# A decoder layer on one core: squares of x from a second copy, the last weights' second token half held back, and sums of activations two tiles at once

## The chip, the cores and the metric

The kernel runs on one core of one Trainium2 chip. The metric is the device time in microseconds of one execution of the program. The core's engines are PE (TensorE, matmuls), DVE (VectorE), ACT (ScalarE), POOL (GpSimd) and SP (SyncE, which here only issues DMAs). Every engine works through its own list of instructions in order and waits on semaphores.

## What is computed

One layer of a hybrid decoder for a sequence of 256 tokens with 2048 channels, all in float32, and a final norm:

```python
h = rms_norm(x, norm_mix_g)
q, k, v, xr, gr, sc_b, sc_c, sc_x, g_pre = split(h @ w_in)
y_a = moba_attention(q, k, v, rel_table) @ w_attn_o
y_b = rg_lru_branch(xr, gr, ...) @ w_lru_o
y_c = (sc_b * causal_conv3(sc_c * sc_x)) @ w_sc_o
g_a, g_b, g_c = split(sigmoid(g_pre + gate_b))
x = x + (g_a * y_a + g_b * y_b + g_c * y_c) @ w_out
h = rms_norm(x, norm_mlp_g)
x = x + square(relu(h @ w_mlp_up)) @ w_mlp_down
return rms_norm(x, final_g)
```

where `rms_norm(x, g) = x * rsqrt(mean(x*x, -1) + 1e-6) * g`. All weights together are about 300 MB.

## The kernel before

**Weights in two parts.** The weights are read once, as 512 KB blocks: 128 partitions x 2 x 512 numbers, which is 256 rows of a matrix by 512 columns. SP loads each into one of nine buffers `raw` (RAW = 9). ACT copies it into `hi` in the type fp32r (line 158), DVE takes the rest `lo` = `raw` - `hi` (line 159); there are five buffers of each (WB = 5). Activations are split in the same way. A product is then three matmuls: hi x hi, hi x lo and lo x hi. For blocks 0 to 7 `first` does the same (lines 206 and 207) and also makes the activations `h`: ACT scales a tile of x by its gains (line 363), DVE forms the rest (line 364). The order of the blocks is a list that is worked out ahead (`jobs`); `ahead` prepares blocks up to LOOK = 3 ahead of the one that is multiplied.

**Two ways to multiply.** `group` ("ws") holds the weights still and streams the activations: four PSUM banks, for every 128 x 128 piece one matmul with 512 columns (line 245) and one with 256 (line 246). The first two groups are `xr0` and `xr1`, over blocks 0 to 7 and 8 to 15; then `qk`. `pair` ("as") holds the activations still and streams 512 columns of weights (line 291), for both halves of the tokens (t = 0 and 1) and two stretches of 512 output channels (gi = 0 and 1). The pairs of the gates (`gt00` to `gt21`, one for each branch and half of the channels), of `w_out` (`wo0`, `wo1`) and of `w_down` (`dn00` to `dn31`) do half of their weights with a scheme of seven products in place of eight. Its steps ("s", numbered 1 to 7) take sums of blocks of weights, which DVE adds (line 186), and sums of activations, which `sums` makes: four steps on DVE (lines 97 to 100), a copy on ACT (`...ch`, line 102) and the rest on DVE (`...cl`, line 103). The plain weights are steps "n". `as_sequence` gives the order of the steps; after step 1 of a pair ACT copies the bank of (0, 0) into `...r1` (line 299, `gt21r` in the rows). `total` (lines 338 and 340, `xr0a` and `xr0b`) adds the two halves of a bank.

**Work beside.** Code that may run later is put into the lists `after` and `side`, from which `a_bit` takes a piece between blocks. Tile, the framework, fixes from the program the order of the instructions on each engine except SP, and adds the waits. Buffers of one tag are a pool: a new tile waits for the last use of the tile whose place it takes. `block` is a pool of 55 tiles of 128 x 512.

**The first norm.** POOL squares the tiles of x and adds them into `sqa`, eight multiplications and seven additions; six matmuls on PE (`pss`, lines 396 and 399) add over the partitions; `rsqrt` works on a tile of 128 x 258. The factor is needed from the evacuation of `xr` on.

**The end.** The final norm of x needs the sum of squares of each token over all channels, so it follows the last pair, `dn31`: ACT squares (line 842), DVE multiplies with the gains (line 843), seven small steps give the factor `r`, and eight scalings (lines 861 and 863) and eight DMAs of 256 KB follow.

Of the kernel before, what the change touches and what calls it, by code (L numbers as in the profile page):

```python
# [47 lines left out]
def as_sequence(nu, nb):  # L48
# [12 lines left out]
    return mixed((1, 2, 3, 4), n2) + mixed((5, 6, 7), n1)  # L61
# [3 lines left out]
def trunk_kernel(ctx, tc, x8, xn, pv, rows, w_in, rel, onehot, w_a, lru_w, w_l, w_s, w_out, w_up, w_down, out2):  # L65
# [70 lines left out]
    for kind, w, g, u0, nu, nb in order:  # L136
# [3 lines left out]
        else:  # L140
            seq = as_sequence(nu, nb)
# [123 lines left out]
    def pair(name, w, g, plain, mix, evac):  # L265
# [9 lines left out]
        def mixed(b, kk, m):  # L275
# [3 lines left out]
            return [x[:, at:at + P] for x in mix[b, kk]]  # L279
# [65 lines left out]
    xb, hl = [], []  # L345
# [576 lines left out]
```

## Time and profile before

| | |
|---|---|
| median of 3 runs (lowest, highest) | 1595.6 us (1593.0, 1595.79) |
| the profiled execution | 1596.78 us |
| its span on the core | 1594.7 us |
| PE busy | 1553.9 us (97%) |
| DVE, ACT, POOL busy | 82%, 55%, 5% |
| mean granted clock of PE | 0.993 of full speed |

The profile is of one execution. Its span is the time from the core's first to its last recorded event; 2.1 us of the execution's time lie around it. Busy shares are means over the whole span; the waits of an engine, and what released it, say where it stood still.

### The profile page before, as it was taken

To read this page: it belongs to the slowest core of one execution; us is meant where nothing else is said; L and a number is where in the kernel's file an instruction comes from. 1 tells how busy PE (TensorE), PEld (TensorE's weight loads), DVE (VectorE), ACT (ScalarE), POOL (GpSimd) and SP (SyncE) were. 2 spreads that over 40 slices of the span, in tenths; PEclk is the share of its full clock that TensorE was granted. 3 is DMA by queue.
4 is the path that set the end of the run, shared out by engine and by line. 5 is a ranking of instruction groups with operands and counts; after the bars stand their busy time and mean duration, and the time that the engine had idled before them with its cause. 6 is when DMAs were issued, how large, how long until landed. Compare 5 with 4: busy or idle time off the path is not lost.

```text
span 1594.7 us, 20814 instructions
## 1 busy us (share of the span) xinstructions
PE 1553.9 (97%) x7694; PEld 1302.7 (82%) x7694; DVE 1300.3 (82%) x1701; ACT 873.8 (55%) x1166; POOL 77.0 (5%) x85
## 2 busy tenths in 40 slices
PE   6999999999999999998999999999999999999996
PEld 5888888878888888786888888888888888888875
DVE  8964576998759886989799778987799679977897
ACT  4544856565545464655456655545555455545554
POOL 6021200000000000200100000000000000000000
PEclk9999999999999999999999999999999999999998
DMA  8665455465754575383754653575466654576353
GB/s 306 199 210 163 155 189 168 146 212 174 259 187 158 205 258 184 119 277 132 251 177 166 239 187 124 198 272 186 155 211 222 201 185 155 197 250 215 127 179 118
DMA packets 86421, 307.67 MB, mean 193 GB/s; under 512 B 10141, under 2 KB 10405, under 8 KB 86320
## 3 DMA queue, kind: packets, MB, share of 16 engines
q1 hardware_dynamic: 82656, 296.57, 55.7%
q0 software_dynamic: 2656, 8.45, 1.8%
q10 hardware_dynamic: 1008, 1.32, 0.3%
q8 instruction: 60, 0.98, 0.3%
q14 instruction: 41, 0.34, 0.1%
HBM read 304.20 MB, written 2.11 MB: 192 GB/s over the span
## 4 chain that ended last, share of the span: by engine, by line
PE 88%; DVE 7%; issue 2%; ACT 1%; DMA 1%; POOL 1%; SPq 0%; ACTq 0%; DVEq 0%; POOLq 0%
PE dn L291 20%; PE up L245 15%; PE gt L291 12%; PE up L246 8%; PE y L291 7%; PE wo L291 5%; PE qk L245 4%; PE v L291 3%; DVE lo L159 2%; PE qk L246 2%; PE sc L245 2%; PE sx L245 2%; DVE raw L186 1%; PE sb L245 1%; PE xr L245 1%
## 5 line engine op out<-in xcount | busy, mean ns | idle before, releaser
L159 DVE TENSOR_TENSOR lo<-raw,hi 128x1024 fp32r<-128x1024 f32 x648 | 775.2, 1223 | 229.6 <-ACT hi L158 221.6
L158 ACT ACTIVATE hi<-raw 128x1024 fp32r<-128x1024 f32 x648 | 664.8, 1055 | 533.2 <-DVE raw L186 105.5
L245 PE MATMUL up<-h,hi 128*128 128x512 f32 x1024 | 362.1, 399 | 0.0
L246 PE MATMUL up<-h,lo 128*128 128x256 f32 x1024 | 287.7, 281 | 0.0
L245 PEld LDWEIGHTS up<-h,hi 128*128 128x128 f32 x1024 | 192.4, 188 | 47.8
L291 PE MATMUL dn<-hi,U 128*128 128x512 f32 x704 | 223.6, 389 | 0.9 <-ACT hi L158 0.9
L246 PEld LDWEIGHTS up<-h,lo 128*128 128x128 f32 x1024 | 193.4, 189 | 0.1
L291 PE MATMUL gt<-hi,h 128*128 128x512 f32 x528 | 170.4, 394 | 7.1 <-ACT gt21r L299 4.0
L291 PEld LDWEIGHTS dn<-hi,U 128*128 128x128 f32 x704 | 132.0, 188 | 29.0 <-ACT hi L158 1.5
L186 DVE TENSOR_TENSOR raw<-raw,raw 128x1024 f32<-128x1024 f32 x128 | 153.7, 1218 | 0.8
L291 PE MATMUL dn<-lo,U 128*128 128x512 f32 x352 | 137.1, 390 | 0.0
L291 PEld LDWEIGHTS gt<-hi,h 128*128 128x128 f32 x528 | 99.5, 189 | 29.9 <-ACT hi L158 5.0
L291 PE MATMUL gt<-lo,h 128*128 128x512 f32 x264 | 103.8, 393 | 0.4 <-DVE lo L159 0.3
L245 PE MATMUL qk<-h,hi 128*128 128x512 f32 x256 | 91.4, 401 | 0.0
L291 PEld LDWEIGHTS dn<-lo,U 128*128 128x128 f32 x352 | 66.1, 188 | 13.9 <-DVE lo L159 0.3
L246 PE MATMUL qk<-h,lo 128*128 128x256 f32 x256 | 71.7, 280 | 0.0
L291 PEld LDWEIGHTS gt<-lo,h 128*128 128x128 f32 x264 | 50.1, 190 | 11.8 <-DVE lo L159 1.6
L245 PEld LDWEIGHTS qk<-h,hi 128*128 128x128 f32 x256 | 48.1, 188 | 12.1 <-ACT hi L158 0.6
L245 PE MATMUL xr<-h,hi 128*128 128x512 f32 x128 | 47.3, 419 | 8.3 <-DVE h L364 8.2
L246 PEld LDWEIGHTS qk<-h,lo 128*128 128x128 f32 x256 | 48.3, 189 | 0.3
L245 PE MATMUL sc<-h,hi 128*128 128x512 f32 x128 | 46.5, 402 | 0.0
L245 PE MATMUL sx<-h,hi 128*128 128x512 f32 x128 | 46.0, 402 | 0.0
(1044 smaller groups left out, 2369.3 us busy)
## 6 DMA issues: line engine op xcount, KB each, us to landing
raw<-in_w_in SPq DMA_DIRECT2D x222, 512.0 KB, 4.4
raw<-in_w_up SPq DMA_DIRECT2D x128, 512.0 KB, 4.4
raw<-in_w_down SPq DMA_DIRECT2D x128, 512.0 KB, 4.4
raw<-in_w_out SPq DMA_DIRECT2D x32, 512.0 KB, 4.7
raw<-in_w_a SPq DMA_DIRECT2D x16, 512.0 KB, 4.6
raw<-in_w_s SPq DMA_DIRECT2D x16, 512.0 KB, 4.9
raw<-in_w_l SPq DMA_DIRECT2D x16, 512.0 KB, 5.0
gb<-in_rows POOLq DMA_DIRECT2D x12, 256.0 KB, 4.8
```

Source lines behind the costliest of these rows:

```text
L158: act.activation(hi, raw, AF.Copy)
L159: dve.tensor_sub(lo, raw, hi.bitcast(F32))
L186: dve.tensor_add(t, t, add)
L245: pe.matmul(ps[j], hi[:, kk, cs], acts[k], start=(k == 0), stop=False)
L246: pe.matmul(ps[j][:, :S], lo[:, kk, cs], acts[k][:, :S], start=False, stop=(k == nk - 1))
L291: pe.matmul(ps[key], hl_[x], w2[y][:, kk], start=key not in begun, stop=end and i == 2, skip_group_check=True)
```

## The change

**Squares of x.** `first` and `start` no longer issue POOL's squares. Ahead of each of the blocks 8 to 15 SP loads a quarter of one half of the tokens of x a second time, tokens along the partitions (`xq`, 128 x 512, 256 KB), and ACT squares it with a running sum along the row (`ss1`). `first_norm` makes the factor on 128 x 2 numbers, and gets it along the other axis by two transposes on PE (`rt`, `pb`). Three empty entries are put into `after`, so that it comes three pieces later.

**Sums.** `sums` takes two tiles of 128 x 512 at once and works on 128 x 2 x 128 in its four steps and on 128 x 1024 after that; `h_sums`, the gated merge and the `up` part call it half as often. Its tiles come from a pool of their own, `six`, with six buffers of 128 x 1024, and `block` has 43 in place of 55.

**Last pair.** In `dn31` the second half of the sequence is sorted: all steps "s", then the plain weights. For the last four weights (LATE = 4) only t = 0 is multiplied at first; t = 1 follows with all four after that. The final norm is done for each t as soon as its four stretches are there, with its own four scalings and output DMAs.

```diff
-NBLK = 55
+NBLK = 43
+SIX = 6
+LATE = 4
...
-    return mixed((1, 2, 3, 4), n2) + mixed((5, 6, 7), n1)
+    end = mixed((5, 6, 7), n1)
+    return mixed((1, 2, 3, 4), n2) + (sorted(end, key=lambda s: s[0] == "n") if late else end)
...
     def sums(name, a1, a2):
 
-        c = block(f"{name}c")
-        c4 = [c[:, i * P:(i + 1) * P] for i in range(4)]
-        dve.tensor_sub(c4[0], a1[:, P:], a2[:, P:])
-        dve.tensor_sub(c4[1], c4[0], a1[:, :P])
-        dve.tensor_sub(c4[2], a1[:, :P], a1[:, P:])
-        dve.tensor_add(c4[3], a2[:, :P], c4[1])
-        hi, lo = block(f"{name}ch", F32R), block(f"{name}cl", F32R)
+        a1, a2 = (a.rearrange("p (k s) -> p k s", k=2) for a in (a1, a2))
+        c, hi, lo = (six.tile([P, 2, 512], dt, tag="six", bufs=SIX, name=f"{name}{n}")
+                     for n, dt in (("c", F32), ("ch", F32R), ("cl", F32R)))
+        c4 = [c[:, :, i * P:(i + 1) * P] for i in range(4)]
+        dve.tensor_sub(c4[0], a1[:, :, P:], a2[:, :, P:])
+        dve.tensor_sub(c4[1], c4[0], a1[:, :, :P])
+        dve.tensor_sub(c4[2], a1[:, :, :P], a1[:, :, P:])
+        dve.tensor_add(c4[3], a2[:, :, :P], c4[1])
         act.activation(hi, c, AF.Copy)
         dve.tensor_sub(lo, c, hi.bitcast(F32))
...
             job = jobs[c]
+            if KT // 2 <= c < KT:
+                t, i = divmod(c - KT // 2, 4)
+                xq.append(block(f"xq{t}{i}"))
+                sp.dma_start(xq[-1], xn[t, :, 512 * i:512 * (i + 1)])
+                act.activation(xq[-1], xq[-1], AF.Square, accum_out=ss1[:, t, i:i + 1])
...
             if what == "n":
-                for t in range(2):
+                held = n >= len(seq) - late
+                for t in range(1 if held else 2):
                     for kk in range(2):
                         product((t, gi), n, plain(2 * unit + kk, t), w2, kk, last[t, gi] == n and kk == 1)
-                keys = [(0, gi), (1, gi)]
+                keys = [(0, gi)] if held else [(0, gi), (1, gi)]
...
+        if late:
+            for n in range(len(seq) - late, len(seq)):
+                for kk in range(2):
+                    product((1, gi), n, plain(2 * seq[n][4] + kk, 1), parts[used[0] - len(seq) + n], kk,
+                            n == len(seq) - 1 and kk == 1)
+            o, op = others[1, gi] if nb else (None, None)
+            rest.append(evac(1, gi, ps[1, gi], got.get(o), op))
...
-            if i % 2:
-                q = sqa if i == 1 else block(f"sq{i}")
-                pool.tensor_mul(q, xb[i // 2], xb[i // 2])
-                if i > 1:
-                    pool.tensor_add(sqa, sqa, q)
...
     def first_norm():
-        pss = small("pss")
-        for m in range(2):
-            pe.matmul(pss[:, :S], ones, sqa[:, m * S:(m + 1) * S], start=(m == 0), stop=(m == 1))
+        v, q, w = (sc8[:, i, :2] for i in range(3))
+        r = rs1[:, S:]
+        dve.tensor_reduce(v, ss1, axis=mybir.AxisListType.X, op=OP.add)
...
+        pb = small("pb")
         for t in range(2):
-            for m in range(2):
-                pe.matmul(pss[:, S + t:S + t + 1], sqa[:, m * S + t * P:m * S + (t + 1) * P], ones[:, :1],
-                          start=(m == 0), stop=(m == 1))
-        rsqrt(rs1, pss[:, :S + 2], S + 2, "n1")
+            rt = block(f"rt{t}")[:, :P]
+            act.activation(rt, ones, AF.Copy, scale=r[:, t:t + 1])
+            pe.transpose(pb[:, t * P:(t + 1) * P], rt, ident)
+        act.activation(rsb, pb[:, :S], AF.Copy)
...
+    def final_norm(t):
+        v, q, n = (nrm[:, t, i:i + 1] for i in range(3))
+        dve.tensor_reduce(v, ss3[:, t], axis=mybir.AxisListType.X, op=OP.add)
+        act.activation(q, v, AF.Sqrt, scale=1.0 / D, bias=warm)
...
+        for i in range(4):
+            o = x2[t, i]
+            if i == 1:
+                act.activation(o, o, AF.Copy, scale=n)
+            else:
+                dve.tensor_scalar(o, o, n, None, op0=OP.mult)
+            (act if i % 2 else sp).dma_start(out2[t, :, 512 * i:512 * (i + 1)], o)
```

How the lists of the engines change at three places. First ACT at the turn from the first eight blocks to the later ones. `raw_...` and `hi_...` are the parts of one block of weights (the number is the tile's), `sc` small constants, `xr0a` the copy in the evacuation of the bank `xr_0`. Before:

```order
L206 ACTIVATE hi_296<-raw_295 128x1024
L426 ACTIVATE sc_177<-sc_177 128x8
L158 ACTIVATE hi_314<-raw_312 128x1024
L338 ACTIVATE xr0a<-xr_0_178 128x256
L158 ACTIVATE hi_352<-raw_350 128x1024
```

In the changed kernel:

```order
L217 ACTIVATE hi_280<-raw_279 128x1024
L439 ACTIVATE sc_167<-sc_167 128x8
L176 ACTIVATE xq_293,ss_78<-xq_293 128x512
L358 ACTIVATE xr0a<-xr_0_168 128x256
L164 ACTIVATE hi_298<-raw_296 128x1024
L176 ACTIVATE xq_334,ss_78<-xq_334 128x512
L358 ACTIVATE xr1a<-xr_1_169 128x256
L164 ACTIVATE hi_339<-raw_337 128x1024
L176 ACTIVATE xq_343,ss_78<-xq_343 128x512
L358 ACTIVATE xr2a<-xr_2_170 128x256
L358 ACTIVATE xr3a<-xr_3_171 128x256
```

The squares of `xq` are new, and `xr0a` to `xr3a`, which wait for PE's matmuls on the first eight blocks, now stand ahead of the `hi` of the next block instead of behind it.

Second, DVE in the pair `gt21`, where the sums of the merged activations for the first half (m0, before: m00 and m01) and the second (m1, before: m10 and m11) are made between the weights. The `raw` rows add two blocks of weights for a later step. Before:

```order
L103 TENSOR_TENSOR m10cl<-m10c,m10ch 128x512
L97 TENSOR_TENSOR m11c<-mf_6547,mf_6558 128x128
L99 TENSOR_TENSOR m11c<-mf_6547 128x128
L98 TENSOR_TENSOR m11c<-m11c,mf_6547 128x128
L186 TENSOR_TENSOR raw_00_6436<-raw_00_6436,raw_10_6761 128x1024
L100 TENSOR_TENSOR m11c<-mf_6558,m11c 128x128
L186 TENSOR_TENSOR raw_00_6454<-raw_00_6454,raw_10_6792 128x1024
L159 TENSOR_TENSOR lo_6765<-raw_00_6436,hi_6764 128x1024
L103 TENSOR_TENSOR m11cl<-m11c,m11ch 128x512
L159 TENSOR_TENSOR lo_6777<-raw_6774,hi_6776 128x1024
L302 TENSOR_TENSOR gt_6695<-gt_10_6677,gt21r_6605 128x512
```

In the changed kernel:

```order
L165 TENSOR_TENSOR lo_6709<-raw_11_6608,hi_6708 128x1024
L315 TENSOR_TENSOR gt_6705<-gt_20_6601,gt_6705 128x512
L108 TENSOR_TENSOR m0cl<-m0c,m0ch 128x1024
L103 TENSOR_TENSOR m1c<-mf_6523,mf_6534 128x2x128
L105 TENSOR_TENSOR m1c<-mf_6523 128x2x128
L104 TENSOR_TENSOR m1c<-m1c,mf_6523 128x2x128
L706 TENSOR_TENSOR gt_6724<-gt_11_6587,gt_6705 128x512
L106 TENSOR_TENSOR m1c<-mf_6534,m1c 128x2x128
L708 SCALAR_TENSOR_TENSOR gt_6724<-gt_6724,rs_166,gb_6481 128x512
L197 TENSOR_TENSOR raw_00_6421<-raw_00_6421,raw_10_6728 128x1024
L108 TENSOR_TENSOR m1cl<-m1c,m1ch 128x1024
L197 TENSOR_TENSOR raw_00_6439<-raw_00_6439,raw_10_6759 128x1024
```

`m0cl`, which before stood far ahead as `m00cl` and `m01cl`, has moved behind the two steps on `gt`, and it, the sums of m1 and `m1cl` lie ahead of the second addition of `raw`. On ACT the copy `gt21r` now stands ahead of `m1ch` (it stood behind `m11ch`). The place that `m0cl` takes in the six buffers is that of `h0ch`.

Third, the end of PE's list. `dn_00` is the bank of t = 0, `dn_10` that of t = 1, `U` the activations that are held still; `hi` and `lo` with one number belong to one block. Before, the last block is:

```order
L291 MATMUL dn_00_13765<-hi_14031,U_13391 128x512
L291 MATMUL dn_00_13765<-lo_14032,U_13391 128x512
L291 MATMUL dn_00_13765<-hi_14031,U_13391 128x512
L291 MATMUL dn_00_13765<-hi_14031,U_13407 128x512
L291 MATMUL dn_00_13765<-lo_14032,U_13407 128x512
L291 MATMUL dn_00_13765<-hi_14031,U_13407 128x512
L291 MATMUL dn_10_13857<-hi_14031,U_13391 128x512
L291 MATMUL dn_10_13857<-lo_14032,U_13391 128x512
L291 MATMUL dn_10_13857<-hi_14031,U_13391 128x512
L291 MATMUL dn_10_13857<-hi_14031,U_13407 128x512
L291 MATMUL dn_10_13857<-lo_14032,U_13407 128x512
L291 MATMUL dn_10_13857<-hi_14031,U_13407 128x512
```

In the changed kernel, from the last block's first matmul:

```order
L303 MATMUL dn_00_13661<-hi_13915,U_13287 128x512
L303 MATMUL dn_00_13661<-lo_13916,U_13287 128x512
L303 MATMUL dn_00_13661<-hi_13915,U_13287 128x512
L303 MATMUL dn_00_13661<-hi_13915,U_13303 128x512
L303 MATMUL dn_00_13661<-lo_13916,U_13303 128x512
L303 MATMUL dn_00_13661<-hi_13915,U_13303 128x512
L303 MATMUL dn_10_13753<-hi_13879,U_13043 128x512
L303 MATMUL dn_10_13753<-hi_13879,U_13059 128x512
L303 MATMUL dn_10_13753<-lo_13880,U_13059 128x512
L303 MATMUL dn_10_13753<-hi_13879,U_13059 128x512
L303 MATMUL dn_10_13753<-hi_13891,U_13075 128x512
L303 MATMUL dn_10_13753<-lo_13892,U_13075 128x512
```

Of the last block only t = 0 stands in its old place; 22 matmuls on `dn_10`, of which six are shown, follow it to the end of the list.

## Rows read from the trace of the kernel before

**Rows 1.** The head of the page: the span, and busy time, share of the span and instructions of each engine.

```profile
span 1594.7 us, 20814 instructions
PE 1553.9 (97%) x7694; PEld 1302.7 (82%) x7694; DVE 1300.3 (82%) x1701; ACT 873.8 (55%) x1166; POOL 77.0 (5%) x85
```

**Rows 2.** PE's waits: the matmuls that waited, what for, us in total, how often, and the longest.

```profile
PE xr L245 <- DVE h L364: 8.2, 1, 8.2
PE xr L246 <- DVE lo L207: 5.5, 4, 2.0
PE gt L291 <- ACT hi L158: 4.5, 7, 1.2
PE gt L291 <- ACT gt21r L299: 4.0, 1, 4.0
PE gt L291 <- DVE lo L159: 2.5, 4, 0.9
```

**Rows 3.** Stretches of the start: us from the span's start, length, busy time of each engine (x instructions), granted clock of PE, share of the DMA engines, GB/s.

```profile
20.00:25.00 5.00, 5.00 (x30) 4.19 (x29) 5.00 (x7) 2.11 (x4) 4.99 (x8) 1.00 1.03 405
25.00:30.00 5.00, 3.13 (x20) 2.47 (x19) 5.00 (x4) 0.00 (x0) 4.84 (x4) 1.00 1.03 338
30.00:35.00 5.00, 3.03 (x17) 2.39 (x17) 4.96 (x7) 0.00 (x0) 2.87 (x3) 1.00 0.60 206
35.00:40.00 5.00, 5.00 (x22) 4.24 (x21) 4.06 (x12) 2.20 (x4) 0.00 (x0) 0.66 0.69 220
```

**Rows 4.** The start by lines: duration in ns (minimum, median, maximum) with the times of the first and the last start, and from the lists of DVE and ACT in time order: start, us, instruction, and in brackets the idle time before it and what ended it.

```profile
L364 DVE SCALAR_TENSOR_TENSOR h<-x,pvt,h x16: 472/1258/1508, 6.8 to 34.3; 128x256 fp32r<-128x256 f32 x16
L207 DVE TENSOR_TENSOR lo<-raw,hi x10: 691/1266/2289, 5.4 to 35.2; 128x1024 fp32r<-128x1024 f32 x6, 128x512 fp32r<-128x512 f32 x4
L371 POOL TENSOR_TENSOR sqa<-sqa,sq x7: 1332/1355/2254, 9.1 to 31.6; 128x512 f32<-128x512 f32 x7
...
6.82 5.10 DVE L364 SCALAR_TENSOR_TENSOR h<-x,pvt,h 128x256 fp32r<-128x256 f32 x4
...
11.33 1.06 ACT L206 ACTIVATE hi<-raw 128x1024 fp32r<-128x1024 f32 x1 [1.35 <-DMA raw<-in_w_in]
35.13 0.21 ACT L426 ACTIVATE sc<-sc 128x8 f32<-128x8 f32 x1 [12.86 <-DVE sc L425]
```

**Rows 5.** PE's list in order of time, its first matmul and the ninth, the first one behind the matmuls of the first norm, and the first of `qk`. A matmul of line 246 (256 columns) follows each of line 245 (512 columns).

```profile
8.19 0.79 PE L245 MATMUL xr<-h,hi 128*128 128x512 f32 x1 [8.19 <-DVE h L364]
10.92 0.54 PE L245 MATMUL xr<-h,hi 128*128 128x512 f32 x1
...
48.43 0.48 PE L245 MATMUL xr<-h,hi 128*128 128x512 f32 x1
...
65.47 0.40 PE L245 MATMUL qk<-h,hi 128*128 128x512 f32 x1
```

**Rows 6.** By line, duration in ns: ACT's square and its read of the running sum, and PE's transposes.

```profile
L842 ACT ACTIVATE sq<-xr x8: 612/630/634, 1522.9 to 1582.0; 128x512 f32<-128x512 f32 x8
L842 ACT ACTIVATION_READ_ACCUMULATOR sq<-xr x8: 183/186/187, 1523.4 to 1582.5; 128x1 f32 x8
L726 PE MATMUL pm<-ident,gt x32: 270/272/328, 727.7 to 809.6; 128*128 128x128 f32 x32
```

**Rows 7.** A stretch of gt00 (columns as in rows 3), and two kinds of steps of `sums` on DVE.

```profile
320.00:330.00 10.00, 7.92 (x30) 4.92 (x29) 10.00 (x11) 5.70 (x7) 0.00 (x0) 1.00 0.15 52
...
734.22 0.28 DVE L97 TENSOR_TENSOR m00c<-mf,mf 128x128 f32<-128x128 f32 x1
738.43 0.68 DVE L103 TENSOR_TENSOR m00cl<-m00c,m00ch 128x512 fp32r<-128x512 f32 x1
```

**Rows 8.** A stretch of gt21, the matmuls on PE that waited there and the one with which they get short again, and ACT's copy of the bank.

```profile
745.00:755.00 10.00, 7.30 (x29) 4.94 (x28) 9.84 (x17) 4.67 (x7) 0.00 (x0) 1.00 0.88 304
...
746.85 0.50 PE L291 MATMUL gt<-lo,h 128*128 128x512 f32 x1 [0.27 <-DVE lo L159]
751.91 0.50 PE L291 MATMUL gt<-lo,h10ch 128*128 128x512 f32 x1 [0.76 <-DVE lo L159]
757.37 0.80 PE L291 MATMUL gt<-hi,h 128*128 128x512 f32 x1 [4.05 <-ACT gt21r L299]
761.81 0.56 PE L291 MATMUL gt<-hi,h10ch 128*128 128x512 f32 x1
...
756.74 0.58 ACT L299 ACTIVATE gt21r<-gt 128x512 f32<-128x512 f32 x1
```

**Rows 9.** The tail in order of time: PE's last matmul, the last small step, and the share of the DMA engines in 40 slices of 1584 to 1595 us.

```profile
1580.75 0.39 PE L291 MATMUL dn<-hi,U 128*128 128x512 f32 x1
...
1584.50 0.16 DVE L856 SCALAR_TENSOR_TENSOR r<-q,r 128x2 f32<-128x2 f32 x1
...
DMA  0000000499999999999999999999997420000000
```

**Rows 10.** Stretches of the last pair, DVE's last two `lo`, and a long run of matmuls in a pair with their count (from the chain that ended last).

```profile
1540.00:1550.00 10.00, 9.33 (x39) 6.83 (x39) 10.00 (x10) 4.50 (x7) 0.00 (x0) 1.00 0.11 29
1560.00:1570.00 10.00, 10.00 (x45) 8.09 (x44) 10.00 (x12) 5.83 (x8) 0.00 (x0) 1.00 0.28 107
...
1574.63 2.35 DVE L159 TENSOR_TENSOR lo<-raw,hi 128x1024 fp32r<-128x1024 f32 x2
...
1324.84 81.83 PE dn L291 x360
```

More of the change, by code (lines that the diff above doesn't have):

```diff
@@ L45, with as_sequence @@
 NB_GATE, NB_OUT, NB_DOWN = 2, 2, 2
-def as_sequence(nu, nb):
+def as_sequence(nu, nb, late):
     n1, n2 = ([("n", 0, 0, i, u) for u in range(2 * nb, nu)] for i in range(2))
@@ L72, in trunk_kernel @@
     blk = ctx.enter_context(tc.tile_pool(name="blk", bufs=1))
+    six = ctx.enter_context(tc.tile_pool(name="six", bufs=1))
     wts = ctx.enter_context(tc.tile_pool(name="wts", bufs=1))
@@ L135, in trunk_kernel @@
     uses = []
-    for kind, w, g, u0, nu, nb in order:
+    last_pair = len(order) - 1
+    for n, (kind, w, g, u0, nu, nb) in enumerate(order):
         if kind == "ws":
@@ L140, in trunk_kernel @@
         else:
-            seq = as_sequence(nu, nb)
+            seq = as_sequence(nu, nb, n == last_pair)
             uses.append(seq)
@@ L263, in group, with pair @@
         after.extend(r for r in rest if r)
-    def pair(name, w, g, plain, mix, evac):
+    def pair(name, w, g, plain, mix, evac, late=0):
         follow("as", w, g)
@@ L278, in mixed @@
             at = (m - 2) * P
-            return [x[:, at:at + P] for x in mix[b, kk]]
+            return [x[:, kk, at:at + P] for x in mix[b]]
         for n, s in enumerate(seq):
@@ L344, in trunk_kernel @@
     pvt = const.tile([P, NPV], F32, name="pvt")
-    xb, hl = [], []
+    xb, hl, xq = [], [], []
+    ss1 = const.tile([P, 2, 4], F32, name="ss1")
     ones = const.tile([P, P], F32, name="ones")
@@ L351, in trunk_kernel @@
     act.activation(warm, ones[:, :1], AF.Exp)
-    sqa = block("sqa")
     def load(eng, i, n):
@@ L475, in evac @@
             b = total(ps, f"xr{g}")
+            if g == 0:
+                after.extend([lambda: None] * 3)
             def rest():
@@ L603, in h_sums @@
         for b in range(NB_GATE):
-            for kk in range(2):
-                a = block(f"ha{b}{kk}")
-                for i in range(2):
-                    h = hl[4 * b + 2 * i + kk].bitcast(F32)
-                    dve.tensor_add(a[:, i * S:(i + 1) * S], h[:, :S], h[:, S:])
-                hm[b, kk] = sums(f"h{b}{kk}", a[:, :S], a[:, S:])
-                yield
+            a = [block(f"ha{b}{i}") for i in range(2)]
+            for i in range(4):
+                h = hl[4 * b + i].bitcast(F32)
+                dve.tensor_add(half(a, i), h[:, :S], h[:, S:])
+            hm[b] = sums(f"h{b}", *a)
+            yield
     beside(h_sums())
@@ L734, in rest @@
                     if gi < NB_OUT:
-                        for kk in range(2):
-                            mm[gi, kk] = sums(f"m{gi}{kk}", *(f[:, kk * S:(kk + 1) * S] for f in mf))
+                        mm[gi] = sums(f"m{gi}", *mf)
                 return rest
@@ L818, in evac @@
                 U.append(o)
-                if gidx >= NB_DOWN or j < 2:
+                if gidx >= NB_DOWN or j < 3:
                     return
                 def rest(gidx=gidx, uf=uf):
-                    um[gidx, j - 2] = sums(f"u{part}{gidx}{j}", half(uf, j - 2), half(uf, j))
+                    um[gidx] = sums(f"u{part}{gidx}", *uf)
                 return rest
@@ L843, in evac @@
                     dve.tensor_mul(o, o, gf[i])
[L844 to L864 removed]
+                    done.append(t)
+                    if done.count(t) == 4:
+                        final_norm(t)
+            pair(f"dn{part}{p2}", w_down, 2 * p2, lambda k, t: in_two(U[k], t), um, evac,
+                 late=LATE if part == PARTS - 1 and p2 else 0)
 def _onehot():
```

45 lines of the change are left out of this document (15 added, 30 removed).

## The prediction

> **What bounds the kernel now.** The header of the page first: TensorE (PE) is busy for 97% of the span, the vector engine (DVE) 82%, the scalar engine (ACT) 55% [rows 1]. So nothing is gained by taking work off DVE or ACT in general; a gain has to be PE waiting less, PE doing less, or the parts before PE's first and after its last matmul becoming shorter. The list of PE's waits says where it waits: 8.2 us before its first matmul, 5.5 us for second parts (`lo`) at the start, 4.5, 4.0 and 2.5 us inside the gate pairs `gt` [rows 2]. The stretches of the start show why PE waits there: from 20 to 35 us DVE is busy all the time, PE is busy 3.13 and 3.03 of 5 us, and right after that the granted clock of a 5 us stretch is 0.66 [rows 3]. Last, the end: PE's last matmul ends at 1581.14, the span at 1594.7; a chain of small steps, eight scalings and eight output DMAs lie between [rows 9].
>
> The profiled execution took 1596.78 us: span 1594.7 plus 2.1 around it. The runs shown have their median at 1595.6, 1.2 below it. I make the sum against 1596.78 and carry the difference over to the median. About 0.2% (3.2 us) is what a measurement of this kernel can tell from no change.
>
> **First norm.** The change removes fifteen GpSimd instructions (seven additions with a median of 1.355 us, eight squares). While they run, DVE's `h` step takes 1258 ns in the median; its shortest, once the last of them has ended, takes 472 ns [rows 4]. So I cost DVE's start anew with 0.45 us per `h` and 1.2 us per `lo`, 2.1 us for one block of weights, against about 3.9 now (two `h` at 1.26 and a `lo` of 1.2 to 2.3). PE needs 5.68 us for two blocks: 48 pairs of matmuls took from 48.43 to 65.47, which is 0.355 us each [rows 5], and two blocks are 16 pairs. 4.2 us of DVE for 5.68 us of PE: PE is then the slower one and stops waiting after its first blocks. Walking through it: the first `h` step starts at 6.82 [rows 4] and ends at about 7.4 with the semaphore, so PE begins 0.8 us earlier than at 8.19; its first 16 pairs take 16 x 0.355 and 1.3 more for the low clock (four pairs from 8.19 to 10.92 [rows 5]) and end at 14.5; three more groups of 16 end at 31.6; two waits of 0.25 and 0.8 us follow, because ACT now has the evacuation `xr0a` ahead of `hi` of block 8 (order shown above) and `xr0a` waits for PE; four groups more and two transposes (0.27 us each at most [rows 6]) end at 55.7. Now the same point, the first `qk` matmul, is at 65.47 [rows 5]. In these 9.8 us are also the six matmuls of `pss`, which go, and the low clock at 35 to 40.
>
> What the new work costs: eight squares on ACT, 0.63 + 0.19 us each by the same operation at the end of the kernel [rows 6]. ACT has nothing to do from 22.3 to 35.1 (its idle time of 12.86 us [rows 4]), so these 6.6 us are covered; were they not, each would push its block by 0.8 us. The copies `xq` are 2.1 MB on SP's queue, each ahead of the block with the same number, behind raw 7. The DMA engines are full up to 25 us (share 1.03, 405 GB/s), and then fall to 0.60 to 0.69 [rows 3]: the copies go into that gap. The small vectors of the norm are ready at about 47.4 by this walk and PE wants them at 51.85, so they are covered by 4.4 us. Not covered is this: GpSimd, without its squares, issues the four `lw` loads (1.1 MB) at about 3 to 7 us instead of 20.4, when the engines are full. Bounds: nothing, if they go in turn behind blocks that PE doesn't wait for; 1.1 MB at 405 GB/s, 2.6 us, if every byte delays a block that PE waits for. I take 1.0, nearer to nothing, since of the blocks that these loads meet only 2 and 3 are wanted at once. The Trainium skill (DMA: Bandwidth & Descriptors, "Issuing engines are not separate DMA queues") says that all queues interleave on the same sixteen engines; by that alone it would be the 2.6. First norm: -9.8 + 1.0 = **-8.8** (bounds -9.8 and -7.2).
>
> **Sums of two tiles at once.** Twelve calls instead of 24. Two old calls cost DVE eight steps and two `lo`: 0.28 and 0.68 by the rows [rows 7], 0.2 and 0.6 from start to start, since each begins a little before the last has ended: 2.8 us. A `lo` of twice the size takes 1.14 from start to start (two together 2.35 [rows 10], one by itself 1.21), so 512 elements more are 0.54 and 128 more 0.135: one new call costs four steps of 0.335 and a `lo` of 1.14, 2.5 us. DVE saves 0.3 per call, or nothing if the three-dimensional form runs slower. Eight of the calls (`up`) lie where PE never waits, so they are worth nothing. Two lie ahead of gt00: there DVE is busy 10.00 of 10 us and PE only 7.92, so PE is bound by it and gets what DVE saves in two calls [rows 7]: **-0.6**; bounds 0, and -2.1 (all that PE loses there). Two lie in gt21. There PE now waits 0.27 + 0.76 + 4.05 us and then works at the low clock until 761.81, ten matmuls in 4.44 us instead of 2.3 (0.227 each, by 81.83 us for 360 [rows 10]): 7.2 us in all [rows 8]. The 4.05 is a wait for ACT's copy `gt21r`, ready at 756.74 + 0.58, which stands on ACT behind the last of the sums. In the new order `gt21r` is ahead, so this wait goes. What is late next: the sums have six buffers of their own, so `m0cl` has to wait on DVE until PE has used `h0ch` for the last time (752.75 by my walk), and behind it on DVE stand the four steps of m1, two steps on `gt` and the addition that makes the next weights. From 752.75: 1.2 + 1.5 + 1.3 + 1.1 gives 757.7 for the addition, 758.7 for its `hi`, 761.1 for its `lo`. PE, by the same walk, wants them from 756.85 on: waits of 1.85, 0.8 and 1.1, 3.8 in all. That leaves 7.2 - 3.8 = 3.4, or 1.3 if the clock falls as it does now. I take **-2.5**; bounds 0 (the new buffers take it all) and -4.5 (no wait at all before the next weights but the second).
>
> **Last pair and tail.** After PE's end T the chain to `r` takes 3.5 us, then eight scalings and 2.1 MB of output, which the DMA engines carry for some 6 us [rows 9]. With the first token half already out, 1.05 MB are left: half the transfer, -3.0. But the pair is a stretch in which DVE has 10.00 of 10 us [rows 10]: the last `lo` ends at 1576.98. Now PE needs it 11 matmuls before T, 2.5 us, at 1578.65, so it is 1.7 us early. In the new order 27 matmuls follow its first use (27 x 0.227 = 6.1 us), and DVE's list before it is as long as it was: T can't be before 1576.98 + 6.1 + 0.1 = 1583.2, 2.1 us later than now; 1.8 to 2.8 with the earlier `raw` additions. So -3.0 + 2.4 = **-0.6** (bounds -1.2 and -0.2). PE would wait in three pieces for `lo`. In 1540 to 1550 PE lost 0.67 us and kept its clock at 1.00; at 25 to 35 it lost 3.8 us and at 35 to 40 the clock was 0.66 [rows 3, 10]. The expected 2 to 3 us lie between the two. The Trainium skill (TensorE: Matmul & The Clock Gate, "A second HAM failure mode: psum-queue depth-cycling") says that frequent short idling makes the clock swing to the half and back without any one long gap; by that rule the low clock comes here. It is a rival below.
>
> **Sum.** -8.8 - 0.6 - 2.5 - 0.6 = -12.5: 1584.3 against the profiled execution, **1583.1** against the median.
>
> **Rivals.**
> *The start is bound by transfers.* Copies and `lw` together are 3.2 MB more in a stretch that is full up to 25 us. For it: `hi` of block 2 already waits 1.35 us for its transfer [rows 4]. Against: 40% of the engines are free after 30 us. Were half of the start's gain lost (4.4 us), the time is 1587.5. Chance 0.15.
> *Six buffers are too few.* If `m0cl` waits for PE and PE for what stands behind it, all of gt21's gain goes and the second pass of it (m1) costs another 1 to 2 us: -12.5 + 2.5 + 1.5, 1587.1. For it: DVE has next to no idle time from 745 to 755 (9.84 of 10 us busy [rows 8]) to make it up. Against: that order takes the 4.05 us wait out for certain. Chance 0.13.
> *The last pair falls to the low clock.* The low stretch of 4.44 us at gt21 cost 2.1 us [rows 8]; the same here: 1585.2. Chance 0.14.
> *Slower: the squares hold ACT.* `hi` of blocks 8 to 15 stands on ACT behind the square of its copy. Copies and blocks are 6.3 MB, queued from about 21 us. PE wants the last at 50; the kernel is slower than now by 0.2% only if it comes 12.5 + 3.2 = 15.7 us late, at 66: a rate under 6.3 MB / 45 us = 140 GB/s. The rows show 206 to 220 where the queue was half empty and 405 where it was full [rows 3], so this is unlikely: 1600 at 135 GB/s. Chance 0.04. At 206 GB/s the last block comes at 52, near the forecast.
> *It hardly does anything*, since PE's start was set by transfers all along (`h` gets faster, PE doesn't): -12.5 + 8.8 + 1, 1592.9. Chance 0.06.
>
> **Numbers.** The forecast has 0.48. All cases except the last two are faster by more than 3.2 us: faster 0.90, the same 0.06, slower 0.04. Range: all gains at their better bound (-9.8, -2.1, -4.5, -1.2) give 1578.0; PE's waits in the gate pairs are 11.0 us [rows 2], 5.1 in gt21 and 2.1 in gt00, and of the 3.8 in the other four one may go with DVE's work: 1577. The rivals reach 1587.5, two of them together 1590. So 1577 to 1590.
>
> **What would show it.** In the new trace: GpSimd nearly idle in the first 40 us, `h` at 0.45 to 0.5 us, PE's waits for `lo` in `xr` under 1.5 us in all, the first `qk` matmul at 56 to 58, no low clock at 35 to 40. No wait of PE for `gt21r`, but one for `hi` or `lo` of about 2 us behind it. PE's last matmul at about 1571.5, the end 10.5 us after it instead of 13.6. It is wrong if `qk` starts after 60 (DMA rows then show `raw` or `xq` landing late), or if PE loses over 5 us in the last pair.

## The result and the profile after

The changed kernel takes 1580.5 us in the median (1579.2 to 1580.7), the kernel before, on the same chip, 1594.3; the ratio is 0.9921 with a 95% interval of 0.9908 to 0.9934: 12.6 us faster, 10.5 to 14.7 (the two medians alone lie 13.8 apart, within that interval). Forecast were 12.5 us, and 1583.1 us in a range from 1577 to 1590. The head of the page and PE's waits in the changed kernel, which answer to [rows 1] and [rows 2]:

```profile
span 1578.4 us, 20748 instructions
PE 1549.1 (98%) x7684; PEld 1300.0 (82%) x7684; DVE 1282.0 (81%) x1649; ACT 875.8 (55%) x1172; POOL 55.5 (4%) x70
...
PE xr L256 <- DVE h L384: 6.8, 1, 6.8
PE gt L303 <- ACT hi L164: 5.6, 8, 1.9
PE dn L303 <- DVE lo L165: 1.9, 3, 0.9
PE gt L303 <- DVE lo L165: 1.4, 2, 0.9
PE xr L256 <- ACT hi L217: 0.9, 1, 0.9
PE xr L257 <- DVE lo L165: 0.4, 1, 0.4
```

The wait for `gt21r` is gone and the 5.5 us for `lo` at the start are 0.4; new are 1.9 us for `lo` in `dn`. The two profiled executions differ by 16.3 us of span (1594.7 and 1578.4), 3.7 us more than the ratio says: the profiled execution of before lay 2.5 us above its median. 2.9 of the 16.3 us lie in two stages whose length differs between executions of one program: 1.6 in the first part of up and 1.3 in gt20 (last section). The places where PE starts a new stage divide the span (each figure to about 0.2 us):

| stage on PE | before, us | after, us | difference | forecast |
|---|---|---|---|---|
| start to the first qk matmul | 65.5 | 55.7 | -9.8 | -8.8 |
| qk to the first gate matmul | 247.6 | 247.5 | -0.1 | 0 |
| gt00 to gt20 and what lies between | 415.5 | 413.1 | -2.3 | -0.6 |
| gt21 | 50.4 | 48.5 | -1.9 | -2.5 |
| y21, wo0, wo1 | 109.5 | 109.5 | 0 | 0 |
| first part of up | 91.7 | 90.1 | -1.6 | 0 |
| dn00 to the last part of up | 516.9 | 517.1 | 0.2 | 0 |
| dn30 and dn31 | 84.0 | 87.1 | 3.0 | 2.4 |
| after PE's last matmul | 13.6 | 9.9 | -3.7 | -3.0 |

The start, in rows that answer to [rows 3], [rows 4] and [rows 5] (by line: least, median and longest time in ns; stretches; PE's first matmul, its next wait and the first of qk):

```profile
L384 DVE SCALAR_TENSOR_TENSOR h<-x,pvt,h x16: 477/479/488, 6.2 to 24.2; 128x256 fp32r<-128x256 f32 x16
...
10.00:15.00 5.00, 4.10 (x25) 3.31 (x23) 1.09 (x4) 2.04 (x4) 0.00 (x0) 1.00 1.03 356
25.00:30.00 5.00, 5.00 (x30) 4.38 (x29) 2.29 (x8) 0.82 (x3) 0.00 (x0) 1.00 1.04 401
30.00:35.00 5.00, 4.61 (x26) 3.51 (x25) 3.33 (x12) 3.95 (x10) 0.00 (x0) 1.00 1.03 398
35.00:40.00 5.00, 5.00 (x30) 4.35 (x30) 4.83 (x13) 5.00 (x12) 0.00 (x0) 1.00 1.04 407
45.00:50.00 5.00, 5.00 (x31) 4.39 (x30) 2.93 (x6) 3.49 (x6) 0.00 (x0) 1.00 1.03 394
...
6.78 0.80 PE L256 MATMUL xr<-h,hi 128*128 128x512 f32 x1 [6.78 <-DVE h L384]
14.97 1.19 PE L256 MATMUL xr<-h,hi 128*128 128x512 f32 x4 [0.90 <-ACT hi L217]
...
55.69 0.39 PE L256 MATMUL qk<-h,hi 128*128 128x512 f32 x1
```

`h` takes 479 ns and never more than 488, PE works through from 15 us on but for one wait of 0.38 us at 33.8, and the low clock at 35 to 40 is gone. The DMA share is over 1 up to 50 us, where it had fallen to 0.60 at 30: the copies fill the gap, and PE has no wait there but that of 0.38 us.

gt21, answering to [rows 8]: PE's waits, three steps of DVE, and two stretches.

```profile
746.84 0.55 PE L303 MATMUL gt<-hi,h 128*128 128x512 f32 x1 [1.92 <-ACT hi L164]
747.78 0.79 PE L303 MATMUL gt<-hi,h 128*128 128x512 f32 x1 [0.40 <-ACT hi L164]
749.08 0.80 PE L303 MATMUL gt<-lo,h 128*128 128x512 f32 x1 [0.50 <-DVE lo L165]
...
740.65 1.23 DVE L108 TENSOR_TENSOR m0cl<-m0c,m0ch 128x1024 fp32r<-128x1024 f32 x1 [0.20 <-PE gt L303]
744.40 1.22 DVE L197 TENSOR_TENSOR raw<-raw,raw 128x1024 f32<-128x1024 f32 x1
746.67 1.22 DVE L197 TENSOR_TENSOR raw<-raw,raw 128x1024 f32<-128x1024 f32 x1
...
745.00:750.00 5.00, 2.27 (x4) 1.30 (x5) 5.00 (x5) 4.43 (x6) 0.83 (x2) 0.71 0.69 238
750.00:755.00 5.00, 5.00 (x15) 3.86 (x15) 5.00 (x7) 2.01 (x3) 0.66 (x2) 0.60 0.87 288
```

And the tail, answering to [rows 9] (the last row is the share of the DMA engines in 40 slices of 1568 to 1578 us):

```profile
1568.16 0.39 PE L303 MATMUL dn<-hi,U 128*128 128x512 f32 x1
...
1571.90 0.16 DVE L825 SCALAR_TENSOR_TENSOR nrm<-nrm 128x1 f32<-128x1 f32 x1
...
DMA  0199999999999530000002999999989995200000
```

The engines carry output twice, for the first half from 1568.3 to 1571.8 and for the second from 1573.3 to 1576.8, where they had carried all of it in one piece behind PE's end.

### The profile page after: what moved, and what is told of

Its sections match the earlier page's. It is cut to its first block, busy times and chain, and to the rows that moved or that the text cites. A ratio compares the mean times of both kernels' runs of the same rounds, so it can differ in the third digit from the quotient of the medians.

```text
span 1578.4 us, 20748 instructions
## 1 busy us (share of the span) xinstructions
PE 1549.1 (98%) x7684; PEld 1300.0 (82%) x7684; DVE 1282.0 (81%) x1649; ACT 875.8 (55%) x1172; POOL 55.5 (4%) x70
## 4 chain that ended last, share of the span: by engine, by line
PE 89%; DVE 6%; issue 2%; DMA 1%; ACT 1%; POOL 1%; DVEq 0%; SPq 0%; ACTq 0%; POOLq 0%
PE dn L303 18%; PE up L256 15%; PE gt L303 13%; PE y L303 8%; PE up L257 8%; PE wo L303 5%; PE qk L256 4%; PE v L303 3%; DVE lo L165 2%; PE qk L257 2%; PE sc L256 2%; PE sx L256 2%; PE xr L256 1%; PE sb L256 1%; DVE raw L197 1%
## 5 line engine op out<-in xcount | busy, mean ns | idle before, releaser
L256 PE MATMUL xr<-h,hi 128*128 128x512 f32 x128 | 44.9, 407 | 7.7 <-DVE h L384 6.8
L256 PE MATMUL sx<-h,hi 128*128 128x512 f32 x128 | 46.1, 403 | 0.0
```

The lines of the kernel that those rows point to most:

```text
L256: pe.matmul(ps[j], hi[:, kk, cs], acts[k], start=(k == 0), stop=False)
```

## The experiments

All ratios are to the kernel before, of runs on the same chip.

**Each part alone.** The kernel before with one part of the change each; the core of each edit, for e1_start:

```diff
+                act.activation(xq[-1], xq[-1], AF.Square, accum_out=ss1[:, t, i:i + 1])
...
-                pool.tensor_mul(q, xb[i // 2], xb[i // 2])
```

for e2_sums:

```diff
+NBLK = 43
+SIX = 6
...
+        c, hi, lo = (six.tile([P, 2, 512], dt, tag="six", bufs=SIX, name=f"{name}{n}")
```

and for e3_last:

```diff
+LATE = 4
...
+    end = mixed((5, 6, 7), n1)
```

> The kernel before with the first part of the change alone (squares on ACT from the second copy, first norm by two transposes). Theory A (the gain of the start is PE no longer waiting for a DVE that POOL slows, and it stays): the first qk matmul at 55.5 to 56 instead of 65.5, h steps at 0.48 us, and the whole kernel 9.5 to 10.5 us faster, ratio 0.9935 to 0.9942. Rival B (later waits take some of it back, since the weights' transfers are now nearer to the engines): qk early but the kernel only 4 to 7 us faster, ratio 0.9955 to 0.9975.

Measured: 1584.4 us, 0.9942 (0.9930 to 0.9955), 9.2 us faster; the first qk matmul at 55.80. Theory A, at the lower end of its gain: what the start gains stays to the end.

> The kernel before with the second part alone (sums of two tiles at once, their six buffers, 43 blocks). Theory A (a gain where PE waited for DVE or ACT in gt00 and gt21, nothing else): 3 to 5 us faster, ratio 0.997 to 0.998, no wait of PE for gt21r, and the up part as long as before. Rival B (the 1.7 us that the first up part is shorter in the changed kernel's trace also come from this part, by where its tiles lie): 5 to 6.5 us faster, up part 0 at 90 us instead of 91.7. Rival C (only the profiled execution shows it): under 2 us.

Measured: 1589.0 us, 0.9968 (0.9958 to 0.9978), 5.1 us faster, the first part of up 91.6 us long. Its waits in gt21 are those of the changed kernel to 0.3 us:

```profile
755.98 0.49 PE L294 MATMUL gt<-hi,h 128*128 128x512 f32 x1 [1.92 <-ACT hi L161]
756.93 0.51 PE L294 MATMUL gt<-hi,h 128*128 128x512 f32 x1 [0.46 <-ACT hi L161]
758.21 0.79 PE L294 MATMUL gt<-lo,h 128*128 128x512 f32 x1 [0.78 <-DVE lo L162]
```

So the wait for `gt21r` goes by this part alone, and these three come by it alone. It is theory A, 0.1 us above its upper end. The up part is not shorter in this execution; that this speaks against rival B is settled only by e3 below, which leaves the sums as they were and has that part at 90.1 us.

> The kernel before with the third part alone (last pair sorted, t = 1 of the last four weights held back, final norm for each half). Theory A (what the tail gains the pair loses to waits for lo): tail after PE's last matmul 9.8 us instead of 13.6, pair dn31 2.5 to 3.5 us longer, in sum 0 to 1.3 us faster, ratio 0.9992 to 1.0. Rival B (the pair's loss in the changed kernel comes from the new pools, not from the order): pair 0 to 1 us longer, 3 us faster in all, ratio 0.998.

Measured: 1592.2 us, 0.9986 (0.9977 to 0.9995), 2.2 us faster. dn30 and dn31 take 87.0 us, the tail 9.9: together 0.7 less than before, as theory A has it. The ratio's 2.2 us have an interval from 0.8 to 3.7, so the stages' 0.7 lie at its edge. Three stages that this part leaves as they were are also shorter than in the trace of before: the first qk matmul comes at 63.28 in place of 65.47, gt20 is 1.4 us shorter and the first part of up 1.6. So much can differ between two executions.

The three alone sum to 16.5 us against 12.6 together. Each has an interval of 1.4 to 2 us to either side, so this may be the measurement.

**POOL's squares put back.**

```diff
             hl.append(t)
+            if i % 2:
+                q = sqa if i == 1 else block(f"sq{i}")
+                pool.tensor_mul(q, xb[i // 2], xb[i // 2])
+                if i > 1:
+                    pool.tensor_add(sqa, sqa, q)
```

> The changed kernel with POOL's fifteen squares and additions put back at the same places, their result not used. Theory A (POOL's work slows DVE's steps on two SBUF operands, and that was the wait): h back at 1.2 us in the median, PE waits for lo and h again, first qk matmul at 62 to 65, the kernel 6.5 to 9 us slower than the changed one, ratio to the kernel before 0.996 to 0.998. Rival B (the gain came from the six matmuls, the order of loads and the new norm): h stays under 0.6 us or PE does not wait, qk at 56 to 57, ratio 0.991 to 0.993.

Measured: 1586.9 us, 0.9954 (0.9940 to 0.9967), 5.3 us slower than the changed kernel by the ratios (7.8 by the spans of the profiled executions); the first qk matmul at 63.3. By line, and PE's wait:

```profile
L386 DVE SCALAR_TENSOR_TENSOR h<-x,pvt,h x16: 470/1256/1517, 6.2 to 33.8; 128x256 fp32r<-128x256 f32 x16
...
L393 POOL TENSOR_TENSOR sqa<-sqa,sq x7: 1329/1361/2148, 8.9 to 31.0; 128x512 f32<-128x512 f32 x7
...
PE xr L257 <- DVE lo L218: 6.4, 4, 2.2
```

`h` is back at 1256 ns while ACT's squares, the transposes and the loads `xq` are as in the changed kernel. So about 7.6 of the 9.8 us at qk hang on POOL working beside DVE. The other 2.2 are no more than executions differ: with the start of the kernel before, qk begins at 65.47 (before), 64.90 (e2) and 63.28 (e3). By the ratios the loss is less than the 6.5 us that theory A has at the least; each has some 2 us of interval to either side. The Trainium skill (SBUF — State Buffer, "SBUF: two separate sides") says that GpSimd and VectorE share a pair of ports, which one of them holds for its whole instruction, where VectorE reads two operands from SBUF; by that rule an `h` of 0.48 us waits for a POOL instruction of about 1.3, and the 1256 ns agree: in e4's trace POOL operations end at 7.60, 8.78 and 10.21 us, and the `h` that began under each ends at 7.88, 9.06 and 10.49, each time 0.28 us later.

**Seven buffers for the sums.**

```diff
-SIX = 6
+SIX = 7
...
-                lg = tmp.tile([P, S], F32, tag="lg", bufs=4, name=f"lgs{h}{t}")
+                lg = tmp.tile([P, S], F32, tag="lg", bufs=3, name=f"lgs{h}{t}")
```

> The changed kernel with seven buffers for the sums instead of six (one of the four buffers lg of the attention given up for the room). m0cl, the sums of m1 and m1cl move ahead of the two steps on gt in DVE's list. Theory A (the waits left in gt21, 1.92 + 0.40 + 0.50 us and a low clock behind them, come from m0cl and m1cl being held until PE is done with the sums of h): these waits fall under 1 us in all, no low clock at 745 to 755, 3.5 to 5 us faster than the changed kernel, ratio to the kernel before 0.988 to 0.990. Rival B (DVE has too much to do there in any order): waits of 2 us or more stay in gt21, at another step, ratio within 0.991 to 0.993.

Measured: 1577.6 us, 0.9907 (0.9894 to 0.9921). gt21 takes 45.0 us in place of 48.5. DVE's `m0cl` and the first step on `gt` behind it, PE's waits in gt21, and the stretch of the old waits:

```profile
726.45 1.23 DVE L108 TENSOR_TENSOR m0cl<-m0c,m0ch 128x1024 fp32r<-128x1024 f32 x1
734.61 0.68 DVE L314 TENSOR_TENSOR gt<-gt,gt21r 128x512 f32<-128x512 f32 x1
...
728.87 0.50 PE L303 MATMUL gt<-lo,h0ch 128*128 128x512 f32 x1 [0.66 <-DVE lo L165]
750.97 0.50 PE L303 MATMUL gt<-hi,h 128*128 128x512 f32 x1 [0.45 <-ACT hi L164]
...
745.00:755.00 10.00, 9.55 (x41) 7.24 (x40) 9.96 (x11) 6.72 (x8) 2.66 (x5) 1.00 0.81 256
```

`m0cl` begins at 726.45, 14 us earlier, and the 2.8 us of waits and the low clock behind them are a wait of 0.66 and one of 0.45 at full clock. Theory A in the stage. By the ratios it is 2.2 us beside the changed kernel, less than theory A's 3.5 to 5, with intervals of 2 us. The 3.5 us of the stage are its upper end: the execution of the changed kernel in the tables had one of the two longest stretches of low clock in gt21. With six buffers the stage took 46.2 us in one trace, 47.5 to 47.8 in six and 48.4 to 48.5 in two (last section), so the seventh buffer is worth 1.2 to 3.5 us there.

**The `lw` loads later.**

```diff
-        for i in range(4):
-            t = block(f"lw{i}")
-            pool.dma_start(t.rearrange("p (g j) -> p g j", g=4), lru_w[4 * i:4 * i + 4].rearrange("g p j -> p g j"))
-            lw.append(t)
...
         pool.dma_start(rdram, rsbuf)
+        for i in range(4):
...
```

> The changed kernel with three of the four lw loads issued behind the small matrix of relative positions, far from the start. Theory A (of the term of 1.0 us for these loads): PE's wait of 0.90 us for hi of block 2 and the transfer behind it go, 0.5 to 1.5 us faster than the changed kernel; DMA share at 10 to 15 us as high as before, since other loads move up. Rival B (other loads take the same place): the wait stays at 0.5 us or more, no difference over 0.5 us.

Measured: 1578.0 us, 0.9914 (0.9899 to 0.9929). One of the four loads is still issued at 3.4 us, the other three far behind the start. From 10 to 15 us PE is busy all the time, where it was 4.10 of 5, and qk begins 1.0 us earlier; ACT can begin with block 2 at 10.81:

```profile
10.00:15.00 5.00, 5.00 (x27) 4.34 (x26) 3.98 (x6) 4.45 (x9) 0.00 (x0) 1.00 1.04 402
...
10.81 1.06 ACT L217 ACTIVATE hi<-raw 128x1024 fp32r<-128x1024 f32 x1 [0.38 <-DMA raw<-in_w_in]
...
54.66 0.39 PE L256 MATMUL qk<-h,hi 128*128 128x512 f32 x1
```

In the changed kernel it is:

```profile
13.87 1.06 ACT L217 ACTIVATE hi<-raw 128x1024 fp32r<-128x1024 f32 x1 [1.64 <-DMA raw<-in_w_in]
```

So the loads delay the transfer of block 2 by 3.1 us. That is theory A for the transfer and for PE's wait. What it is worth in time is less clear: 1.1 us by the ratios, with intervals of 2 us. In eight traces with the loads early qk begins between 55.3 and 56.1, and PE's wait for `hi` of block 2 is 0.4 to 0.9 us in five and not there in three, e12 among them, which is the same program as the changed kernel. In the two with the loads late (e6 and e11) it begins at 54.66 and 55.23. Between the means lie 0.7 us.

**How much is held back, and in what order.**

The first line in e7_late2, with 0 in e8_late0 and e9_old0 and 1 in e10_old1; the second in e9_old0 and e10_old1:

```diff
-LATE = 4
+LATE = 2
...
-            seq = as_sequence(nu, nb, n == last_pair)
+            seq = as_sequence(nu, nb, 0)
```

> The changed kernel with LATE = 2 instead of 4. Theory A (PE's end is set by DVE's last lo and the matmuls that follow its first use: 15 instead of 27, 2.7 us less, while the earlier weights' t = 1 fills PE before it; the tail gets longer only if the first half's outputs are still on the way when the second half's start): PE's end 1 to 2 us earlier than with 4, tail 1 to 2 us longer, within 1 us of the changed kernel. Rival B (the waits for lo shift one to one): PE's end stays, tail longer, 1 to 2 us slower.

> The changed kernel with LATE = 0: the pair in its old order, nothing held back, but the final norm still made for each half with its own outputs. Theory A (held weights give the tail 3.7 us and cost the pair 3.0): pair dn31 as long as in the kernel before (waits of 0.7 to 1.1 us), tail 12 to 13.5 us after PE's end, in sum 0 to 1 us slower than the changed kernel. Rival B (most of the tail's gain comes from the norm being made for each half): tail 10.5 to 11.5 us, 1.5 to 2.5 us faster than the changed kernel.

> The changed kernel with the last pair in its old order and nothing held back; the final norm is still made for each half. Theory A (the pair's 3.0 us are lost by the sorted order alone, since it is 86.9 to 87.1 us from the first matmul of dn30 to PE's end with 4, 2 or 0 held weights): dn30 and dn31 take 84.0 us again, tail 11 to 12.5 us, 0.5 to 1.5 us faster than the changed kernel. Rival B (the shorter lists of the sums and the norm for each half cost the pair something too): 85 us or more, no gain.

> The changed kernel with the last pair in its old order and LATE = 1: only the last weight's second half is held back. Theory A (six matmuls, 1.4 us, cover a part of the first half's norm): pair 84.0 to 84.3 us, tail 10.6 to 11.4 us, 1 to 2 us faster than the changed kernel. Rival B (both halves' small steps interleave on DVE and ACT and delay each other): tail 12 us or more, 0 to 1 us faster.

What was written ahead of e8 has a mistake: the sorted order hangs on the pair's place, not on LATE, so it stayed, and the run shows the sorted order with nothing held back. e9 is the run that was meant. All measured values, from the traces and the medians:

| kernel | order, held | dn30 and dn31, us | tail, us | sum | ratio |
|---|---|---|---|---|---|
| before | old, 0, one norm | 84.0 | 13.6 | 97.6 | 1 |
| e9 | old, 0 | 84.0 | 12.0 | 96.0 | 0.9916 |
| e10 | old, 1 | 84.0 | 12.0 | 96.0 | 0.9913 |
| e8 | sorted, 0 | 86.9 | 12.0 | 98.9 | 0.9945 |
| e7 | sorted, 2 | 87.0 | 10.7 | 97.7 | 0.9925 |
| changed | sorted, 4 | 87.1 | 9.9 | 96.9 | 0.9921 |

The norm for each half gives the tail 1.6 us; holding back gives it 1.3 with two weights and 2.1 with four, nothing with one, and costs the pair 0.2 at most; the sorted order costs 2.9 to 3.0. e7 fits neither of its theories: PE's end stays (rival B), the tail is 0.8 longer, not 1 to 2, and the time is within 1 us of the changed kernel's, as theory A has it. e9 confirms theory A of the pair; e10, with its tail of 12.0, is nearer to rival B. By the ratios only e8 stands apart from the others, and its trace also has the longer gt20 and the longer first part of up, which no order of the last pair touches; so it is the stages that tell the rows apart. PE's last matmul in e9 and the stretch in which the sorted order has two of its waits, and below it that stretch of the changed kernel:

```profile
1566.44 0.39 PE L303 MATMUL dn<-hi,U 128*128 128x512 f32 x1
...
1550.00:1560.00 10.00, 10.00 (x45) 8.11 (x44) 10.00 (x12) 8.05 (x11) 0.00 (x0) 1.00 0.00 0
```

```profile
1550.00:1560.00 10.00, 9.01 (x37) 6.50 (x36) 10.00 (x12) 7.83 (x11) 0.00 (x0) 1.00 0.00 0
```

**All that helped.** Seven buffers, late loads, the old order, LATE = 1:

> The changed kernel with seven buffers for the sums, three lw loads late, the old order of the last pair and LATE = 1 together. If the three effects lie apart and add (3.4 in gt21, 1.0 at the start, 1.5 at the end), 5 to 6.5 us faster than the changed kernel, ratio to the kernel before 0.9875 to 0.989; if they meet the same limit, under 4 us.

Measured: 1575.3 us (1574.4 to 1575.4), 0.9883 (0.9866 to 0.9899); the changed kernel beside it 1580.9, so 5.5 us faster than that. In the trace gt21 takes 44.9 us, qk begins at 55.2, and the last pair and the tail take 96.0 together. So the effects add as far as intervals of 2 us can tell.

**The changed kernel again.**

> The changed kernel as it is, beside the others on this chip. Theory A: 1578 to 1581 us and ratio 0.991 to 0.993. For the first up part: if the pair of matmuls takes 0.347 us in it by a property of this program, it takes 90.1 us again; if it is chosen in each execution anew, it may take 91.7.

Measured: 1580.9 us, 0.9921 (0.9906 to 0.9936). The first part of up takes 91.8 us in this execution (last section).

## Why the prediction was right, point by point

The sum of 12.5 against 12.6 is closer than its terms. As measured in this trace, and without what comes with the execution, they are 9.8, 1.0, 1.9 and 0.7, together 13.4. That POOL held DVE at the start, that `gt21r` was waited for, and that the tail carries its output in one piece was read rightly; that the errors of the sizes nearly cancel was luck.

**The start, -8.8 forecast, -9.8 in the trace, 9.2 in e1.** The reason holds: with POOL's work put back the wait is back (e4). The walk came out at 55.7 and so did the kernel, but by errors that cancel. PE began at 6.78, not at 7.4: the walk took DVE's first `h` at 6.82 from the one trace of before, while e2 and e3, with the same start, have it at 6.24 and 6.27, and the changed kernel at 6.24. And the walk to 55.7 was without the loads of `lw`, for which 1.0 us was added; in this execution they cost PE a wait of 0.90 us for `hi` of block 2, in others less or nothing (e6). The Trainium skill's rule of interleaving queues (DMA: Bandwidth & Descriptors, "Issuing engines are not separate DMA queues") agrees with the transfers: block 2 came 3.1 us later with the loads, even more than the 2.6 of the bound. As a bound on PE's time 2.6 was too high, since PE wanted the block only at about 14 to 15 us and noticed the last 0 to 0.9 us of the delay. The claim that the copies go into a gap of the DMA engines is right, but the gap is full: a share of 1.03 until 50 us leaves no room for more.

**Sums, -3.1 forecast.** gt21: the chain is the one that was walked through, `m0cl` (held by the buffers) before the additions of `raw`, and the waits 1.92, 0.40 and 0.50 for 1.85, 0.8 and 1.1. The clock did fall behind them, to 0.71 and 0.60, so the stage gained 1.9, near the lower of the two values. That hangs on the execution: in one without the low clock (e8) it gained 4.2, in six with a shorter one 2.6 to 2.9. So 2.5, chosen between the two values, is near the middle of what was found, but it was chosen between two clocks that the forecast had no way to tell apart. (The steps of that walk add to 757.85, not 757.7; it changes no wait by more than 0.2.) That the buffers hold it was settled by one more of them (e5). In the other gates the forecast was 0.6 and 2.3 were found, but only 1.0 of it is the change: gt00 takes 44.8 to 44.9 us in every trace with the old sums and 43.8 to 43.9 in every one with the new, its waits fell by 0.6, and 0.6 was too little by 0.4. The other 1.3 are in gt20, whose waits are 3.5 us in before and 2.4 in the changed kernel. They come with the execution: e12, the changed kernel again, has gt20 as long as before (47.5 us), and e3, with the old sums, has it as short as the changed kernel (46.1).

**Last pair and tail, -0.6 forecast, -0.7 in the trace.** The two terms are both 0.6 us too small and cancel. The pair: the place of the wait was named wrongly. The bound went by the last `lo` and the 27 matmuls behind its first use. But that `lo` was ready in time, the last wait is at 1556.45, 12.1 us before the end, and the pair is as long with no matmul held back (e8): what costs 3.0 us is the sorted order. It puts three additions of `raw` in a row on DVE, 35 to 33 us before PE's end, where the old order has two there and two some 17 us before the end. With it come three waits for `lo` of 0.90, 0.49 and 0.50 us, each with some tenths more until matmuls come again at their old rate. The first comes right behind the three additions; how they lead to the other two, 15 and 18 us later, is not shown. The tail: half the bytes were counted, 3.0; but with the norm for each half alone it is 1.6, and holding back four weights makes it 3.7.

**Rivals.** No transfer held the start beyond those 0.9 us; the sixth buffer was the limit in gt21 but not worse than what it replaced; the clock stayed at 1.00 in the last pair with 1.9 us of listed waits, so the rule of the Trainium skill on short idling (TensorE: Matmul & The Clock Gate, "A second HAM failure mode: psum-queue depth-cycling") did not come true there, while in gt21 the clock fell; ACT's squares held nothing.

## What to carry to other kernels

A second engine that is "free" may slow the engine that is the bound, even where both have their own work: look at the duration of the same instruction with and without the other engine at work before costing it. A ring of buffers that is a size too small shows as a wait on a producer that has nothing to do with the data, and one more buffer is a cheap test. Where two edits come in one piece (sorted order and holding back), undo them one by one: one lost 3.0 us and the others won 3.7. And a stage's gain in one execution is not yet the change's: gt20 got 1.3 us shorter and the first part of up 1.6 in the pair of traces compared here, and both go back and forth between executions of one program.

## What the runs showed of the hardware

**Two rates of the same matmuls.** In e12, the same program as the changed kernel, the first part of up took 91.8 us, and 90.1 in the first execution: PE works without a wait in both. The clock is 1.00 in both; a pair of matmuls takes 0.353 us from start to start in the one and 0.347 in the other through the whole part. Rows of e12 (a stretch of gt20 with its two waits, matmuls of up with least, median and longest time, and the first run of dn, which begins where up ends):

```profile
655.00:660.00 5.00, 3.35 (x13) 2.55 (x14) 3.92 (x8) 3.08 (x6) 1.95 (x2) 1.00 0.09 16
...
655.77 0.49 PE L303 MATMUL gt<-hi,h 128*128 128x512 f32 x1 [1.02 <-ACT hi L164]
657.15 0.50 PE L303 MATMUL gt<-lo,h1ch 128*128 128x512 f32 x1 [0.88 <-DVE lo L165]
...
L256 PE MATMUL up<-h,hi x1024: 389/398/481, 875.4 to 1483.7; 128*128 128x512 f32 x171
...
967.17 81.83 PE dn L303 x360
```

And of the changed kernel:

```profile
655.00:660.00 5.00, 3.20 (x10) 2.32 (x11) 3.93 (x8) 3.23 (x6) 1.93 (x2) 0.84 0.08 11
...
655.93 0.50 PE L303 MATMUL gt<-hi,h 128*128 128x512 f32 x1 [1.03 <-ACT hi L164]
657.30 0.50 PE L303 MATMUL gt<-lo,h1ch 128*128 128x512 f32 x1 [0.87 <-DVE lo L165]
...
L256 PE MATMUL up<-h,hi x1024: 389/396/473, 874.3 to 1481.0; 128*128 128x512 f32 x171
...
964.39 81.87 PE dn L303 x360
```

So these 1.6 us come with the execution, not with the change. Of the fourteen traces eight have the shorter part, e3 with the old sums among them, and six the longer, before among them. The other three parts of up run at 0.353 us a pair in all fourteen. What sets the rate is open.

**The same wait, another clock.** The same rows show PE's two waits in gt20, 1.02 and 0.88 against 1.03 and 0.87 us, with a granted clock of 1.00 in one execution and 0.84 in the other. In the changed kernel the seven slow matmuls behind them filled the time until the next `hi` was there, and PE did not wait for it. In e12 PE kept its clock, waited 1.19 us for that `hi`, and the low clock came behind this wait; the kernel before does the same (last row):

```profile
663.88 0.50 PE L303 MATMUL gt<-hi,h1ch 128*128 128x512 f32 x1 [1.19 <-ACT hi L164]
665.00:670.00 5.00, 5.00 (x15) 3.83 (x16) 5.00 (x6) 3.57 (x4) 0.00 (x0) 0.66 0.49 139
...
674.91 0.51 PE L291 MATMUL gt<-hi,h10ch 128*128 128x512 f32 x1 [1.19 <-ACT hi L158]
```

gt20 takes 47.5 us in the five traces with the low clock behind the last waits, and 46.1 in the five with it behind the first two; in the other four it has no low clock and takes 46.1 too. In gt21 the three waits of 2.6 to 3.2 us in all were followed by no slow matmul in e8, by six or seven in e2, e4, e6, e7, e9 and e10, and by twelve in the changed kernel's two traces; the stage then took 46.2, 47.5 to 47.8, and 48.4 to 48.5 us. So waits of this size may or may not be followed by the low clock, what it costs depends on whether PE would have waited for something else meanwhile, and a forecast can only give it a chance.
